# Gate and up projections as seven block products in a two-layer decoder trunk

## The chip, the cores and the metric

The kernel runs on one core of a Trainium2 chip. The metric is device time in microseconds (us) of one execution; the median of several runs is compared. The profile is of one further execution. Its engines are TensorE (PE, with PEld for its weight loads), VectorE (DVE), ScalarE (ACT), GpSimd (POOL) and SyncE (SP), which issues the loads.

## The reference

A decoder trunk of two layers on 512 tokens of width 1024, in float32. Each layer is a mixer (attention beside a convolution or a gated MLP) and a SwiGLU feed-forward network (FFN), each behind an RMS norm and with a residual. Only the FFN changes:

```
def swiglu(h, w_gate, w_up, w_down):          # h 512 x 1024, F = 2816
    gate = jnp.einsum('bsd,df->bsf', h, w_gate)
    up = jnp.einsum('bsd,df->bsf', h, w_up)
    return jnp.einsum('bsf,fd->bsd', jax.nn.silu(gate) * up, w_down)

h = h + swiglu(rms_norm(h, ffn_norm_g[layer]), ffn_w_gate[layer], ffn_w_up[layer], ffn_w_down[layer])
```

After the second layer the result goes through a last RMS norm.

## The kernel before

The residual stream is kept transposed: `h[k]`, k = 0 to 7, holds 128 features on the partitions and 512 tokens along the columns. Every float32 product is made of three fp32r products: each operand is split into a high part (a rounding copy on ScalarE) and a low part (a subtraction on VectorE), and hi·hi, hi·lo and lo·hi are added up in a PSUM bank (`acc3`, lines 181 to 187, and `mac` inside `tok_gemm`, lines 241 to 248).

The norm is deferred. `residual` (line 349) adds a product to `h[n]`, and `norm_tile` (line 292) at once splits g·h into `xh[n]` and `xl[n]`; the squares are summed in `nacc`. The scale itself comes later: `norm_a` sums the squares over features with eight short matmuls, and `norm_b` spreads the result over the partitions by transposes into `R`, by which every product is multiplied when it is read out of PSUM.

Weights arrive as one stream `ws` of 182 blocks of 128x1024 (512 KB) in the order of use. `dma_block` loads, three blocks ahead; `prep_unit` splits half a block (128x512, four weight tiles), three units ahead, with ScalarE for hi and, in the FFN, VectorE for lo (in the first mixer GpSimd makes lo).

The FFN (`ffn`) goes over 22 tiles of 128 hidden features. For each it makes the gate product over eight k tiles in one bank, then the up product in another, 24 matmuls of 512 columns each, feature-major: weights are stationary and tokens move, so that the hidden tile comes out with features on the partitions. `act` multiplies by `R`, applies silu, multiplies, and splits the hidden tile into `hh` and `hl`. When all 22 are there, the down projection follows: in layer 0 output tile by output tile over all 22 (528 matmuls), with `residual` and the split for the next mixer behind each; in layer 1 in `last_down`, token-major (`tok_gemm`), in two halves of 512 output columns, while `turn_h` transposes `h` between the matmuls; the last norm and the stores end the kernel.

TensorE runs in the written order; the other engines' orders are found by a planner at compile time. `Seq` puts dependent steps of the mixers between weight products at estimated times.

Of the kernel before, what the change touches and what calls it, by code (L numbers as in the profile page):

```python
# [10 lines left out]
def _warn_once_fixed(msg, *args, **kwargs):  # L11
# [12 lines left out]
P = 128  # L24
S = 512
# [54 lines left out]

def order_ffn_in():
    return [(w, k, f) for f in range(NF) for w in range(2) for k in range(KT)]


def order_down(layer):
    if layer == 0:
        return [(k, n) for n in range(8) for k in range(NF)]
    return [(k, 4 * half + j) for half in range(2) for k in range(NF) for j in range(4)]
# [23 lines left out]
NBLK = 182  # L112
TK = dict(schedule_with_timeline_sim=True)
# [4 lines left out]
def trunk_kernel(ctx: ExitStack, tc: tile.TileContext, xT, ws, cols, sinks, sgu_g, sgu_b,  # L118
# [23 lines left out]
    def dma_block():  # L142
        b = st["dma"]
        raw = wpool.tile([P, 1024], F32, name="raw", bufs=RAW_AHEAD)
        nc.sync.dma_start(raw, ws[b])
        raws[b] = raw
        st["dma"] += 1

    def prep_unit():
# [11 lines left out]
        if half:  # L161
            del raws[b]
            if st["dma"] < NBLK and st["dma"] <= b + RAW_AHEAD:
                dma_block()

    def next_unit():
        u = st["tile"] // 4
        while st["prep"] < min(2 * NBLK, u + PREP_AHEAD + 1):
            prep_unit()
# [19 lines left out]
    # ---- the order on TensorE: products of weights run on, steps that wait for other engines  # L189
    # are put between them when their operands should be there ----  # L190
# [158 lines left out]
    def residual(n, ps, gname):  # L349
        V.tensor_add(h[n], h[n], ps)  # L350
        norm_tile(n, gname)
# [26 lines left out]
    def pt_av(items, vap, rl, dst, banks, line="V", ta="TA", ao="AO"):  # L378
        """items: (unit, column AP of P, key block, first, last)."""
# [46 lines left out]
    # ================= layer 0 mixer =================  # L426
    with ExitStack() as mx:
# [18 lines left out]
        def conv_tile(j, pool_taps):  # L446
            """The first taps: products on ScalarE, summed on GpSimd; the others on VectorE in PSUM."""
# [24 lines left out]
        # GLU pairs  # L472
        def glu(j, pa, pb):
# [4 lines left out]
            # a * sigmoid(b) = a * (tanh(b / 2) + 1) / 2; the half is in the taps  # L478
# [9 lines left out]
        # what is done with a product once the norm's scale is known  # L488
# [37 lines left out]
        # keys: the high part of a head on both halves of the partitions, the low part on its own;  # L526
        # queries: high and low part stacked, so that one pass gives (q_hi + q_lo) k_hi
# [578 lines left out]
```

## Time and profile before

| | us |
|---|---|
| median of 3 runs (lowest to highest) | 1154.53 (1154.25 to 1156.39) |
| span of the profiled execution, first to last instruction | 1148.2 |
| own time of the profiled execution | not listed |
| TensorE busy | 1116.0 (97%) |
| VectorE, ScalarE, GpSimd busy | 596.3, 478.2, 172.8 |

The median lies 6.3 us above the span, for what comes ahead of the first and behind the last instruction. A busy TensorE says that matmuls were under way, not how fast they went: one is shown with 0.39 us while the next starts earlier, so the distance from start to start is the price of a matmul. The granted clock is shown as a share of 2.4 GHz; its other level is 1.2 GHz.

### The profile page before, as it was taken

Reading aid. Unit: us, or ns where it says so; the run is one execution under the profiler, and the core shown is the slowest. Engines: PE = TensorE matmul, PEld = TensorE weight load, DVE = VectorE, ACT = ScalarE, POOL = GpSimd, SP = SyncE. Lnnn points to the kernel's source line nnn. Section 1 sums busy time; section 2 is a strip of 40 time slices with the busy share of each in tenths; the row PEclk is TensorE's granted clock in tenths of the full one; section 3 lists DMA queues with packets and bytes.
Section 4 is the critical chain, followed back from the end, with each engine's and each line's share of the span. In section 5 each row is a group of like instructions: output and inputs, shape, how many; then the busy total and the mean of one; then the engine's idle time right before and its main releaser. Section 6 shows DMA issues by size and latency. Waiting matters only on the chain.

```text
span 1148.2 us, 13412 instructions
## 1 busy us (share of the span) xinstructions
PE 1116.0 (97%) x5132; PEld 911.2 (79%) x5132; DVE 596.3 (52%) x999; ACT 478.2 (42%) x848; POOL 172.8 (15%) x138
## 2 busy tenths in 40 slices
PE   6989899999999999999999999999999999999997
PEld 4867678888888888888887878788888888888886
DVE  6889776544444444333347545664454444432323
ACT  4577666433333333323346644444333333333323
POOL 4788654000000000000024100000000000000100
PEclk9989899999999999999999999999999999999999
DMA  5211112223223322322522111232222322332321
GB/s 212 85 62 56 37 37 92 93 95 106 93 92 98 105 91 92 110 93 92 166 91 71 40 37 52 80 107 88 96 92 95 107 92 92 104 100 91 106 96 74
DMA packets 31281, 103.92 MB, mean 91 GB/s; under 512 B 3568, under 2 KB 4464, under 8 KB 31216
## 3 DMA queue, kind: packets, MB, share of 16 engines
q1 hardware_dynamic: 31216, 103.06, 26.8%
q8 instruction: 40, 0.66, 0.2%
q14 instruction: 25, 0.20, 0.1%
HBM read 100.95 MB, written 2.10 MB: 90 GB/s over the span
## 4 chain that ended last, share of the span: by engine, by line
PE 89%; DVE 5%; POOL 2%; issue 2%; ACT 1%; DMA 0%; SPq 0%; POOLq 0%; ACTq 0%; DVEq 0%
PE bank L184 23%; PE bank L185 22%; PE bank L186 22%; PE bank L245 5%; PE bank L247 4%; PE bank L246 4%; PE bank L404 2%; PE bank L390 1%; PE bank L910 1%; POOL yc L458 1%; PE bank L909 1%; PE bank L567 1%; POOL w_lo L134 1%; PE bank L566 1%; DVE bank L462 0%
## 5 line engine op out<-in xcount | busy, mean ns | idle before, releaser
L157 ACT ACTIVATE w_hi<-raw 128x512 fp32r<-128x512 f32 x364 | 229.4, 631 | 461.7 <-PE bank L185 364.1
L184 PE MATMUL bank<-xh,w_hi 128*128 128x512 f32 x912 | 363.0, 398 | 6.6 <-ACT xh L296 6.6
L134 DVE TENSOR_TENSOR w_lo<-raw,w_hi 128x512 fp32r<-128x512 f32 x321 | 226.1, 705 | 268.7 <-ACT w_hi L157 268.5
L185 PE MATMUL bank<-xl,w_hi 128*128 128x512 f32 x912 | 359.3, 394 | 1.8 <-DVE xl L297 1.7
L186 PE MATMUL bank<-xh,w_lo 128*128 128x512 f32 x912 | 358.5, 393 | 0.0
L184 PEld LDWEIGHTS bank<-xh,w_hi 128*128 128x128 f32 x912 | 173.6, 190 | 44.1 <-ACT xh L296 6.6
L185 PEld LDWEIGHTS bank<-xl,w_hi 128*128 128x128 f32 x912 | 173.7, 190 | 39.2 <-DVE xl L297 4.0
L186 PEld LDWEIGHTS bank<-xh,w_lo 128*128 128x128 f32 x912 | 173.5, 190 | 36.4
L245 PE MATMUL bank<-w_hi,hh 128*128 128x512 f32 x176 | 69.4, 394 | 0.1
L247 PE MATMUL bank<-w_hi,hl 128*128 128x512 f32 x176 | 68.6, 390 | 0.0
L246 PE MATMUL bank<-w_lo,hh 128*128 128x512 f32 x176 | 68.5, 389 | 0.0
L184 PE MATMUL bank<-hh,w_hi 128*128 128x512 f32 x176 | 68.5, 389 | 0.0
L185 PE MATMUL bank<-hl,w_hi 128*128 128x512 f32 x176 | 68.5, 389 | 0.0
L186 PE MATMUL bank<-hh,w_lo 128*128 128x512 f32 x176 | 68.5, 389 | 0.0
L134 POOL TENSOR_TENSOR w_lo<-raw,w_hi 128x512 fp32r<-128x512 f32 x43 | 59.3, 1379 | 47.4 <-ACT w_hi L157 42.0
L756 DVE TENSOR_TENSOR gb<-bank,R 128x512 f32<-128x512 f32 x44 | 30.4, 691 | 64.7 <-PE bank L186 64.7
L754 DVE TENSOR_TENSOR ga<-bank,R 128x512 f32<-128x512 f32 x44 | 30.4, 692 | 63.6 <-PE bank L186 62.8
L458 POOL TENSOR_TENSOR yc<-yc,prod 128x512 f32<-128x512 f32 x44 | 59.3, 1348 | 8.6 <-ACT prod L457 7.3
L850 POOL TENSOR_SCALAR_AFFINE_SELECT wT<-wT 128x1024 f32<-128x1024 f32 x1 | 1.1, 1097 | 360.8 <-DMA wT<-in_spat_wT 360.8
L462 DVE SCALAR_TENSOR_TENSOR bank<-cp,cc,bank 128x512 f32<-128x512 f32 x72 | 54.0, 750 | 1.2
L346 ACT ACTIVATE hh<-gb 128x512 fp32r<-128x512 f32 x44 | 27.8, 632 | 61.5 <-DVE gb L757 61.4
L825 POOL TENSOR_TENSOR xh<-xh,xl 128x512 f32<-128x512 f32 x4 | 5.7, 1454 | 297.7 <-ACT sq L810 297.7
(175 smaller groups left out, 1344.8 us busy)
## 6 DMA issues: line engine op xcount, KB each, us to landing
raw<-in_ws SPq DMA_DIRECT2D x181, 512.0 KB, 3.4
h<-in_xT SPq DMA_DIRECT2D x8, 256.0 KB, 6.2
out_y<-xh SPq DMA_DIRECT2D x8, 256.0 KB, 2.2
raw<-in_ws SPq DMA_DIRECT2D x2, 256.0 KB, 3.5
ropeC<-in_rope_c SPq DMA_DIRECT2D x2, 256.0 KB, 4.1
ropeS<-in_rope_s SPq DMA_DIRECT2D x2, 256.0 KB, 5.1
wT<-in_spat_wT SPq DMA_DIRECT2D x1, 512.0 KB, 6.2
xl<-in_fin_g SPq DMA_DIRECT2D x2, 256.0 KB, 3.7
```

The source lines that it names most:

```text
L134: eng.tensor_tensor(out=out, in0=a, in1=b, op=ALU.subtract)
L157: A.activation(hi, src, AF.Copy)
L184: T.matmul(ps, hi, xh, start=start, stop=False)
L185: T.matmul(ps, hi, xl, start=False, stop=False)
L186: T.matmul(ps, lo, xh, start=False, stop=stop)
L245: T.matmul(ps[t], xh[:, c], hi, start=(k == 0), stop=False)
L246: T.matmul(ps[t], xh[:, c], lo, start=False, stop=False)
L247: T.matmul(ps[t], xl[:, c], hi, start=False, stop=(k == last))
L458: G.tensor_add(yc[j], yc[j], p)
L462: V.scalar_tensor_tensor(acc, src, w, acc, op0=ALU.mult, op1=ALU.add)
L754: V.tensor_mul(g, pg, R)
L756: V.tensor_mul(u, pu, R)
```

## The change

The gate and up products of a group of four hidden tiles (512 features; the last group has two) become one block product: tokens 0 to 255 and 256 to 511 are the two row blocks, the two halves of the 1024 input features the inner blocks, gate and up the two column blocks. Strassen's scheme in Winograd's form makes it from seven products instead of eight. The sums of activation blocks (S1 to S4) are made once a layer by `sums`, and those of weight blocks (T1 to T4) once a group: T1 and T3 on GpSimd, T2 and T4 on VectorE, in place in the loaded blocks. The sums of products are taken partly in PSUM (banks are added to by a second product after a copy of their first state) and partly on VectorE. The products are token-major, the split activations stationary, and the weights move with 512 columns (256 in the last group).

The hidden features so come out with tokens on the partitions, and `turn` transposes them for the down projection. That is now made group by group, added to `h` each time, between the second and third product of the next group; the last two groups go together at the end, in layer 1 in `last_down`. The norm's scale is a per-token column, so `norm_b` is not called in the FFN. Weights of the FFN's first part no longer pass through `prep_unit`: they have eight buffers of their own (`raw2`, of which the scaled activations take four at first), and are split 1024 columns at a time into three pairs of buffers. `residual` ahead of the FFN no longer splits g·h; the FFN does. The diff's removal of comments is left out below, as are the layout of the weights in memory and the small edits of the stream.

```diff
+GROUPS = [list(range(4 * g, min(4 * g + 4, NF))) for g in range((NF + 3) // 4)]
+BLOCKS = ((0, 0), (1, 0), (1, 1), (0, 1))
+EARLY_N = 3
...
-    def residual(n, ps, gname):
+    def residual(n, ps, gname=None):
         V.tensor_add(h[n], h[n], ps)
-        norm_tile(n, gname)
+        if gname:
+            norm_tile(n, gname)
+        else:
+            norm_sq(n)
...
+    PRODUCTS = (("B11", "A11", 0), ("T1", "S1", 1), ("T2", "S2", 0), ("B22", "S4", 1),
+                ("T3", "S3", 0), ("B21", "A12", 2), ("T4", "A22", 0))
...
+            def operand(name, q, src=None):
...
+                A.activation(hi, src, AF.Copy)
+                sub(V, lo, src, hi)
...
+            def sums(q, x1, x2):
+                a11, a21, a12, a22 = x1[:, :, :256], x1[:, :, 256:], x2[:, :, :256], x2[:, :, 256:]
+                s1, s2, s3, s4 = [scr.tile([P, 2, 256], F32, name=x) for x in ("ga", "gb", "ga", "gb")]
+                sub(V, s1, a22, a21)
+                operand("S1", q, s1)
+                V.scalar_tensor_tensor(s2, s1, -1.0, a11, op0=ALU.mult, op1=ALU.subtract)
+                operand("S2", q, s2)
+                V.scalar_tensor_tensor(s4, s2, -1.0, a12, op0=ALU.mult, op1=ALU.subtract)
+                operand("S4", q, s4)
+                sub(V, s3, a11, a21)
+                operand("S3", q, s3)
+                operand("A12", q, a12)
+                operand("A22", q, a22)
...
+                    x = xg[kh, q] = fp.tile([P, 2, S], F32, name="raw2", bufs=8)
+                    for i in range(2):
+                        k = 4 * kh + 2 * q + i
+                        A.activation(x[:, i, :], h[k], AF.Copy, scale=col(gname, k))
+                    if kh == 0:
+                        operand("A11", q, x[:, :, :256])
+                    else:
+                        sums(q, xg[0, q], x)
...
+            def source(g, name, q):
...
+                    into, more, eng = {"T1": ("B11", "B12", G), "T2": ("T1", "B22", V),
+                                       "T3": ("B12", "B22", G), "T4": ("T2", "B21", V)}[name]
+                    t, other = source(g, into, q), source(g, more, q)
+                    eng.tensor_add(t, t, other)
...
+            def prep_op():
...
+                hi = fp.tile([P, 1024], F32R, name="w2h", bufs=3)
+                lo = fp.tile([P, 1024], F32R, name="w2l", bufs=3)
+                A.activation(hi, src, AF.Copy)
+                sub(V, lo, src, hi)
...
+            def product(g, p, ps, start):
...
+                        for t in range(2):
+                            c = slice(t * P, (t + 1) * P)
+                            out = ps[t][:, :w]
+                            T.matmul(out, xh[:, j % 2, c], wh, start=(start and j == 0), stop=False,
+                                     skip_group_check=True)
+                            T.matmul(out, xh[:, j % 2, c], wl, start=False, stop=False, skip_group_check=True)
+                            T.matmul(out, xl[:, j % 2, c], wh, start=False, stop=(j == 3),
+                                     skip_group_check=True)
...
+            def turn(g, src, half):
...
+                for t in range(2):
+                    pt = bank(6 + t)
+                    for i in range(n):
+                        T.transpose(pt[:, i * P:(i + 1) * P], src[t][:, i * P:(i + 1) * P], ident)
+                    pv = pt[:, :n * P].rearrange("p (f c) -> p f c", f=n)
+                    c = slice((2 * half + t) * P, (2 * half + t + 1) * P)
+                    A.activation(hh[:, :, c], pv, AF.Copy)
+                    sub(V, hl[:, :, c], pv, hh[:, :, c])
...
+                    if prev is not None and p == 0:
+                        turn(g - 1, prev["u2"], 0)
+                    if prev is not None and p == 1:
+                        turn(g - 1, prev["p5"], 1)
+                    product(g, p, banks[b], p in (0, 1, 5))
+                    if p == 1:
+                        if g == 0:
+                            norm_a(7)
+                        elif g < last:
+                            for n in range(8):
+                                pd = bank(6 + n % 2)
+                                down(g - 1, n, pd, True, True)
+                                V.tensor_add(h[n], h[n], pd)
...
+                        if p == 0:
+                            A.activation(p1, ps[t], AF.Copy)
+                        elif p == 1:
+                            A.activation(p5, ps[t], AF.Copy, scale=-1.0)
+                        elif p == 2:
+                            A.activation(u2, ps[t], AF.Copy, scale=-1.0)
+                        elif p == 3:
+                            sub(V, u2, u2, ps[t])
+                        elif p == 4:
+                            sub(V, p5, p5, ps[t])
+                        elif p == 5:
+                            V.tensor_add(p1, p1, ps[t])
+                            A.activation(p1, p1, AF.Silu, scale=r[0])
+                            V.scalar_tensor_tensor(u2, u2, r[0], p1, op0=ALU.mult, op1=ALU.mult)
+                        else:
+                            A.activation(g2, ps[t], AF.Silu, scale=r[1])
+                            V.scalar_tensor_tensor(p5, p5, r[1], g2, op0=ALU.mult, op1=ALU.mult)
+                    if layer == 1 and g == last and p in (4, 5, 6):
+                        turn_h(p - 4)
```

## Rows read from the trace of the kernel before

**Rows 1.** The page: busy time by engine, granted clock in 40 slices (tenths).

```profile
PE 1116.0 (97%) x5132; PEld 911.2 (79%) x5132; DVE 596.3 (52%) x999; ACT 478.2 (42%) x848; POOL 172.8 (15%) x138
...
PEclk9989899999999999999999999999999999999999
```

**Rows 2.** Windows of the gate and up stages; columns stand in the first line.

```profile
core 0: us, PE busy (x) PEld busy (x) DVE busy (x) ACT busy (x) POOL busy (x), PEclk, DMA share, GB/s
...
199.20:452.00 252.80, 252.80 (x1124) 209.48 (x1124) 121.74 (x188) 89.64 (x143) 2.13 (x2) 1.00 0.29 97
...
776.00:1018.00 242.00, 242.00 (x1077) 200.51 (x1075) 115.11 (x178) 86.20 (x136) 1.01 (x1) 1.00 0.29 98
```

**Rows 3.** Timeline of TensorE (start, duration), feature-major; 27 triples apart.

```profile
540.46 0.39 PE L184 MATMUL bank<-hh,w_hi 128*128 128x512 f32 x1
...
558.82 0.39 PE L184 MATMUL bank<-hh,w_hi 128*128 128x512 f32 x1
```

**Rows 4.** The same view, token-major in the last down projection; 11 triples apart.

```profile
1124.95 0.39 PE L245 MATMUL bank<-w_hi,hh 128*128 128x512 f32 x1
...
1132.43 0.39 PE L245 MATMUL bank<-w_hi,hh 128*128 128x512 f32 x1
```

**Rows 5.** The same view around the norm's broadcast, eight transposes.

```profile
787.95 1.05 PE L339 MATMUL bank<-ident,rc 128*128 128x128 f32 x8
788.76 0.48 PE L184 MATMUL bank<-xh,w_hi 128*128 128x512 f32 x1
789.08 0.39 PE L185 MATMUL bank<-xl,w_hi 128*128 128x512 f32 x1
```

**Rows 6.** The same view, score matmuls of 256 columns in the first mixer.

```profile
91.58 0.38 PE L567 MATMUL bank<-kl,qs 64*128 64x256 f32 x1
91.89 0.38 PE L566 MATMUL bank<-khh,qs 128*128 128x256 f32 x1
```

**Rows 7.** The same view around four transposes of h.

```profile
1019.80 0.60 PE L798 MATMUL bank<-ident,h 128*128 128x128 f32 x4
1020.15 0.48 PE L245 MATMUL bank<-w_hi,hh 128*128 128x512 f32 x1
1020.47 0.39 PE L246 MATMUL bank<-w_lo,hh 128*128 128x512 f32 x1
```

**Rows 8.** Groups by line and form: total, mean ns, idle before, by releaser.

```profile
L157 ACT ACTIVATE w_hi<-raw 128x512 fp32r<-128x512 f32 x364 | 229.4, 631 | 461.7 <-PE bank L185 364.1 <-PE bank L247 80.7 <-issue 8.1
...
L913 DVE CUSTOM_DVE_ANT_0 Pm<-bank,mask 128x512 f32<-128x512 f32 x8 | 5.4, 688 | 1.8 <-PE bank L910 1.7
...
L913 DVE CUSTOM_DVE_ANT_0 Pm<-bank,mask 128x256 f32<-128x256 f32 x8 | 3.3, 422 | 2.6 <-PE bank L910 2.3
```

**Rows 9.** Timeline of VectorE at the first layer's FFN entry.

```profile
189.75 1.79 DVE L319 TENSOR_TENSOR nacc<-nacc,sq 128x512 f32<-128x512 f32 x1
...
193.31 1.33 DVE L319 TENSOR_TENSOR nacc<-nacc,sq 128x512 f32<-128x512 f32 x1
...
202.05 0.68 DVE L319 TENSOR_TENSOR nacc<-nacc,sq 128x512 f32<-128x512 f32 x1
202.65 0.68 DVE L134 TENSOR_TENSOR w_lo<-raw,w_hi 128x512 fp32r<-128x512 f32 x1
203.25 0.74 DVE L297 SCALAR_TENSOR_TENSOR xl<-h,cc,xh 128x512 fp32r<-128x512 f32 x1
```

**Rows 10.** Timeline of GpSimd in the same stretch.

```profile
189.67 1.31 POOL L134 TENSOR_TENSOR w_lo<-raw,w_hi 128x512 fp32r<-128x512 f32 x1 [2.11 <-ACT w_hi L157]
192.80 1.30 POOL L134 TENSOR_TENSOR w_lo<-raw,w_hi 128x512 fp32r<-128x512 f32 x1 [1.81 <-ACT w_hi L157]
```

**Rows 11.** Windows ahead of the two FFNs; columns as in rows 2.

```profile
760.00:776.00 16.00, 16.00 (x72) 13.24 (x71) 10.01 (x15) 7.31 (x12) 0.00 (x0) 1.00 0.29 98
...
188.00:199.20 11.20, 11.20 (x50) 9.19 (x50) 11.14 (x15) 7.75 (x14) 4.09 (x4) 1.00 0.23 71
```

**Rows 12.** The page: loads of weight blocks, KB each, us to landing.

```profile
raw<-in_ws SPq DMA_DIRECT2D x181, 512.0 KB, 3.4
```

**Rows 13.** Window and timeline of TensorE behind a wait in the first mixer.

```profile
66.00:70.00 4.00, 1.77 (x5) 1.15 (x5) 3.94 (x10) 3.63 (x8) 4.00 (x4) 0.59 0.16 40
...
69.82 0.63 PE L185 MATMUL bank<-xl,w_hi 128*128 128x512 f32 x1
70.25 0.63 PE L186 MATMUL bank<-xh,w_lo 128*128 128x512 f32 x1
```

More of the change, by code (lines that the diff above doesn't have):

```diff
@@ L112 @@
 NBLK = 182
+SIZES = (14, 8, 44, 22, 20, 8, 44, 22)
+STARTS = [sum(SIZES[:i]) for i in range(len(SIZES) + 1)]
+STREAM = [b for i in range(len(SIZES)) if i % 4 != 2 for b in range(STARTS[i], STARTS[i + 1])]
 TK = dict(schedule_with_timeline_sim=True)
@@ L784, in last_down, with hidden, temps @@
-    def last_down(hid):
+            fp = fx.enter_context(tc.tile_pool(name="ffn", bufs=1, reuse_waits="tile"))
+            last = len(GROUPS) - 1
+            gname = f"ffn_g{layer}"
+            hid = {}
+            def hidden(g):
+                end = "z" if g == last else ""
+                hid[g] = [fp.tile([P, len(GROUPS[g]), S], F32R, name=f"h{x}{end}") for x in "hl"]
+            def temps():
+                return {"p1": [scr.tile([P, S], F32, name="ga") for _ in range(2)],
+                        "p5": [scr.tile([P, S], F32, name="gb") for _ in range(2)],
+                        "u2": [fp.tile([P, S], F32, name="ta", bufs=2) for _ in range(2)],
+                        "g2": [fp.tile([P, S], F32, name="tb", bufs=2) for _ in range(2)]}
@@ new lines, in ffn @@
+            xg = {}
+            for kh in range(2):
+                for q in range(2):
+                    x = xg[kh, q] = fp.tile([P, 2, S], F32, name="raw2", bufs=8)
[6 more added lines that the diff above has]
+                        sums(q, xg[0, q], x)
@@ new lines, in ffn, with block @@
+            base = STARTS[4 * layer + 2]
+            order = [(g, p, q) for g in range(last + 1) for p in range(7)
+                     for q in range(2 if len(GROUPS[g]) == 4 else 1)]
+            fs = dict(block=0, prep=0, take=0)
+            blocks, made, ops = {}, {}, {}
+            def block(g, name, q):
+                nq = 2 if len(GROUPS[g]) == 4 else 1
+                want = 8 * g + BLOCK_OF[name] * nq + q
+                while fs["block"] <= want:
+                    raw = fp.tile([P, 1024], F32, name="raw2", bufs=8)
+                    nc.sync.dma_start(raw, ws[base + fs["block"]])
+                    blocks[fs["block"]] = raw
+                    fs["block"] += 1
+                return blocks[want]
@@ new lines, in ffn @@
+            if gnext is not None:
+                pd = {n: bank(n) for n in range(EARLY_N)}
+                for n in range(EARLY_N):
+                    down(last - 1, n, pd[n], True, False)
+                    if n < 2:
+                        turn(last, prev["u2" if n == 0 else "p5"], n)
+                for n in range(8):
+                    if n < EARLY_N:
+                        down(last, n, pd[n], False, True)
+                    else:
+                        pd[n] = bank(n % 6)
+                        down(last - 1, n, pd[n], True, False)
+                        down(last, n, pd[n], False, True)
+                    residual(n, pd[n], gnext)
+            else:
+                hidden(last)
+                xs2 = [(hid[g][0][:, i, :], hid[g][1][:, i, :]) for g in (last - 1, last)
+                       for i in range(len(GROUPS[g]))]
+                last_down(xs2, lambda k: turn(last, prev["u2" if k == 0 else "p5"], k) if k < 2 else None)
@@ new lines, in trunk_kernel, with turn_h, last_down @@
+    ht_ = []
+    def turn_h(part):
+        if not ht_:
+            ht_.extend([keep.tile([P, S], F32, name=f"xh{2 * t + f}") for f in range(2)] for t in range(NQ))
+        for i in ((0, 1, 2), (3, 4, 5), (6, 7))[part]:
+            f, t = divmod(i, NQ)
+            pt = bank(6 + i % 2)
+            for j in range(4):
+                T.transpose(pt[:, j * P:(j + 1) * P], h[4 * f + j][:, t * P:(t + 1) * P], ident)
+            A.activation(ht_[t][f], pt, AF.Copy)
+    def last_down(hid, each):
```

130 lines of the change are left out of this document (74 added, 56 removed).

## Prediction

> **What bounds the kernel now.** I read the first part of the page, then the windows by stage, then the timeline of TensorE, because the question is whether any time in the two SwiGLU stages is not TensorE's. TensorE is busy for 97% of the span, VectorE for 52%, GpSimd for 15%, at the full clock almost everywhere [rows 1]. In the windows of the gate and up products TensorE has no gap at all: 252.80 of 252.80 us and 242.00 of 242.00 us, with VectorE at 48% and GpSimd idle but for one or two instructions [rows 2]. So these stages last as long as their matmuls do.
>
> The price of a matmul is the distance between starts, since the shown 0.39 us overlap. In a run of feature-major products 27 triples (hi·hi, hi·lo, lo·hi) take from 540.46 to 558.82 us: 0.680 us a triple, 0.2267 us a matmul of 512 columns [rows 3]. Token-major ones, as the change uses, go at the same rate: 11 triples from 1124.95 to 1132.43 us, 0.680 us [rows 4]. Their form costs nothing.
>
> **What the products save.** Before, a layer has 22 tiles x 2 matrices x 8 k tiles x 3 = 1056 matmuls, 239.4 us. After, a block product is 4 k tiles x 2 token tiles x 3 = 24 matmuls, and a group has seven. Five groups of four tiles: 840 of 512 columns, 190.4 us. The last group has two tiles: 168 of 256 columns. No uniform stream of that width is in the trace. Eight transposes of 128 columns before a full-width matmul take 0.81 us, 0.10 each [rows 5]; 512 columns take 0.227, which is 0.213 for the columns at 2.4 GHz and 0.013 over. I take 0.107 + 0.013 = 0.120 us, 20.2 us in all, between bounds of 0.10 (16.8 us) and 0.227 (38.1 us). A row of 256 columns at 0.31 us exists [rows 6], but there full-height and half-height weights alternate, which the change never does; it is only a far upper end. A layer goes from 239.4 to 210.6 us: **-28.8 each, -57.6 us in all** (between -64 and -22).
>
> **What TensorE gets to do instead.** The hidden tiles come out with tokens on the partitions and have to be turned: per full group 16 transposes in two calls of `turn`. The transposes of `h` now show the price: four take 1019.80 to 1020.15, 0.35 us, and the first matmul behind them has 0.32 instead of 0.23 us to the next start, so 0.44 us per four [rows 7]. Eight in a row: 0.81 and 0.09, as the broadcast of the norm shows [rows 5]. That makes 0.9 x 10 + 0.44 x 2 = 9.7 us a layer: **+19.4 us**. The broadcast itself (`norm_b`) leaves both FFNs: 0.90 x 2, **-1.8 us**. The down projection keeps its 528 matmuls a layer; only their order changes. `turn_h` keeps its 32 transposes, but three in a row go through two PSUM banks and wait for ScalarE's copies: +1. TensorE's own balance is -57.6 + 19.4 - 1.8 + 1 = **-39.0 us**.
>
> **Who feeds it now.** The weights of a product are 128x1024 pieces, split into hi on ScalarE and lo on VectorE; a piece feeds 12 matmuls, 2.72 us. VectorE takes 0.688 us at 512 columns and 0.422 at 256 [rows 8]: 1.04 ns a column, so 1.22 us at 1024. ScalarE at 0.63 us for 512 needs at most 1.26, and is half idle. Per full group VectorE then has 14 splits (17.1), four sums T2 and T4 (4.9), six readings of PSUM (4.1), four gated products (3.0, at 0.75 as the three-operand split of `xl` in [rows 9]) and four splits behind the transposes (2.8): 31.9 us beside 39.9 us of products and transposes. Groups 1 to 4 also contain 21.8 us of down matmuls, in which VectorE has only 16 instructions of 0.69. Three buffers let VectorE run two pieces ahead, 5.4 us less the 2.5 us of a split. On average that holds, and starts of 512-column instructions lie 0.60 us apart in a queue [rows 9], so 31.9 is on the high side.
>
> Against it stands GpSimd, which makes T1 and T3. While a GpSimd subtraction ran from 189.67 for 1.31 us, a VectorE addition of two SBUF operands started at 189.75 and took 1.79 us; at 192.80 and 193.31 the same, 1.33 us. Undisturbed it takes 0.68 [rows 9, 10]. Both times VectorE ended 0.55 us behind GpSimd's end: it stood still until GpSimd was through. The Trainium skill, "SBUF — State Buffer", section "SBUF: two separate sides", says so: the port pair that both share is an exclusive lock for the whole instruction, against a VectorE instruction with two SBUF inputs. By that rule every lo split and every operand sum is exposed to every T1 and T3; if such instructions ran freely side by side, the stall term below would be near half. The trace agrees with the rule.
>
> T1 and T3 are four additions of 1024 columns a group. From 1.31 us at 512 [rows 10] I take 2.6 us each (1.3 if most were fixed), 10.4 us a group. In groups 1 to 4, T3 can run under the down matmuls; T1 falls at the group's start, where the readings of two products and a turn come together: about 5.3 us of VectorE work and 2.6 of GpSimd per 5.4 us of matmuls. Two pieces ahead hide most of it. I take 0.7 us of stall at each of the ten group changes, 7 us (0 to 3 us each), and 1 us in each narrow last group, where a product is only 2.9 us long: 2 us.
>
> **Group 0** is the weak place; no down product gives time back. VectorE also makes the sums of the activations there: per half 10 instructions of 0.69 and the split of A11, 15.2 us a layer. Without them it has 29.1 us before the first turn, with them 44.3, and GpSimd up to 10.4 more, against 38.1 us of matmuls. Before group 0 begins VectorE is not free: 10.01 of 16 us busy at the second layer's entry, 11.14 of 11.20 at the first [rows 11]. What leaves it there is the split of eight `xl` tiles. The last residual lands only after the first matmul of the FFN could start; S1, S2 and S4 of the second half hang on it, one after the other. B22's loads also wait for buffers that the scaled activations hold, and a load takes 3.4 us [rows 12]. With some 8 us done ahead and half of GpSimd's time beside PSUM reads, 44.3 + 5 - 8 = 41.3 against 38.1, and order adds to it: I take 4 us at the second layer and 6 at the first, where weights may also wait for the mixer's memory: 10 us (2 to 25).
>
> Stalls: 7 + 2 + 10 = **+19 us**. Sum: -39.0 + 19 = **-20.0 us**, and the span goes from 1148.2 to 1128.2 us. The own time of the profiled execution is not listed; the median of the timed runs is 6.3 us above its span, which I carry over: **1134.5 us**. The 8 to 10 us of ScalarE work that group 0 adds for scaling and splitting cost nothing, because ScalarE is busy 42% of the span; with no cover they would lengthen the 10 us term.
>
> **Rivals.**
> 1. *Everything hidden.* The look-ahead absorbs the lock and the entries. Stalls 0 to 9 us; 1115.5 to 1124.5 us. For it: VectorE's average load of 80% in the products and the 0.60 us spacing [rows 9]. Against it: 11.14 of 11.20 us at the first entry [rows 11].
> 2. *Slower: the port bounds the products.* Each T1 and T3 holds VectorE for its full 2.6 us and look-ahead does not recover it. A full group then needs 31.9 + 10.4 = 42.3 against 39.9 us; group 0 44.3 + 10.4 = 54.7 against 38.1. That is 16.6 + 5 x 2.4 = 28.6 us a layer, 57.2 in all: -39.0 + 57.2 = +18.2, 1172.7 us. It decides from 19.5 us of stall a layer. For it: the two locked additions [rows 9, 10]. Against it: the down matmuls between, during which VectorE catches up.
> 3. *The narrow group is no cheaper.* Its 168 matmuls take 0.227 us each like wide ones: 2 x 17.9 = +36 us, less the 2 us of stall that they then hide, 1168 us; half way, at 0.17 us, 1152. For it: only the 256-column row [rows 6]. Against it: the transposes at 0.10 us [rows 5, 7].
>
> **How the numbers follow.** The forecast's case (stalls of 10 to 30 us, 1125 to 1145 us) gets 0.50, rival 1 0.27, rival 2 from its point on 0.13, rival 3 0.06, half of it on either side, and 0.04 lies on the line. A change of 0.2% (2.3 us) is about what a measurement of this kernel can tell from none. Faster: 0.50 + 0.27 + 0.03 = 0.80; within 0.2%: 0.04; slower: 0.13 + 0.03 = 0.16. The range for 8 in 10 goes from 1112, half way from the sum without stalls (1115.5) to the same with narrow matmuls at 0.10 us (1109), to 1156, where rival 2 has just overtaken the gain; the likeliest case's own is 1125 to 1145.
>
> **What would show it.** Right: 840 matmuls a layer 0.227 us apart and 168 at 0.12; pieces of 1024 columns at 1.2 us on VectorE; TensorE idle mostly in the first 45 us of each FFN, waiting for lo splits or sums; VectorE splits beside GpSimd's additions stretched to 2 or 3 us. Wrong: TensorE without gaps there (rival 1), gaps in every group at its start (rival 2), the last group at 0.2 us a matmul (rival 3). What would upset all of it is an idle stretch long enough that the granted clock falls: between 66 and 70 us, with TensorE busy for 1.77 of 4.00 us behind a wait for VectorE, it was 0.59 on average, that is partly at 1.2 GHz, and matmuls of 512 columns started 0.43 us apart, from 69.82 to 70.25 [rows 13].

## Result, and the profile after

The changed kernel takes 1227.11 us (median of 5 runs, 1219.61 to 1227.53) against 1154.25 us: a ratio of 1.0624 [1.059, 1.0659] (in brackets the 95% interval, here and below), slower. The forecast was 1134.5 us with 0.80 on faster. The profiled execution has a span of 1217.5 us (own time 1219.61, the shortest of the five), 69.3 more than before.

The page of the kernel after, the lines that answer to [rows 1]:

```profile
PE 1111.9 (91%) x5196; PEld 905.9 (74%) x5196; DVE 839.0 (69%) x1105; ACT 573.0 (47%) x932; POOL 317.6 (26%) x182
...
PEclk9989998899999999999999999988999999999999
```

TensorE was busy for 97% and is now for 91%; the clock, without a dip there in [rows 1], dips in slices 7 and 8 and 27 and 28, where the two FFNs begin. The windows of the two FFNs, from the mixer's last matmul to the last down matmul or the end, answer to [rows 2]:

```profile
core 0: us, PE busy (x) PEld busy (x) DVE busy (x) ACT busy (x) POOL busy (x), PEclk, DMA share, GB/s
197.20:594.60 397.40, 360.30 (x1635) 297.15 (x1634) 287.25 (x305) 172.89 (x243) 72.82 (x23) 0.95 0.26 88
810.58:1217.50 406.92, 363.44 (x1665) 300.63 (x1664) 280.69 (x298) 176.87 (x254) 81.55 (x31) 0.95 0.25 86
```

Before, the first FFN lasted 360.9 us without a gap. Now TensorE is busy for about as long (360.3), at a mean clock of 0.95, and stands still for 37 us besides. From the last matmul of a mixer to that of the FFN's down projection, and in layer 1 to the last matmul of all, the kernel before takes 360.92 + 365.16 = 726.1 us and this one 397.19 + 399.89 = 797.1: +71.0 us. The mixer between them takes 215.9 and 216.0. The first mixer ended anywhere from 196.8 to 204.0 us in the profiled executions of this study, so experiments are compared below by this sum of the two FFNs ("FFN sum") as well as by their times.

The sum of the prediction without stalls would be 726.1 - 39.0 = 687.1; the stalls are 110 us, not 19. They lie in two places, in both layers: from the mixer's last matmul to the end of group 0, and at every change of group. The page's groups name the instructions that stretch (mean ns of one behind the comma):

```profile
L147 DVE TENSOR_TENSOR w2l<-raw,w2h 128x1024 fp32r<-128x1024 f32 x154 | 227.1, 1475 | 103.2 <-ACT w2h L864 103.1
L854 POOL TENSOR_TENSOR raw<-raw,raw 128x1024 f32<-128x1024 f32 x44 | 134.6, 3065 | 583.7 <-DVE w2l L147 582.3
```

**A change of group.** The three timelines of layer 0 from the last product of group 2 into group 3 (GpSimd, VectorE, TensorE), and a window behind the wait.

```profile
394.61 5.65 POOL L854 TENSOR_TENSOR raw<-raw,raw 128x1024 f32<-128x1024 f32 x2 [56.03 <-DVE w2l L147]
401.41 5.58 POOL L854 TENSOR_TENSOR raw<-raw,raw 128x1024 f32<-128x1024 f32 x2 [1.16 <-DVE w2l L147]
```
```profile
393.30 1.23 DVE L147 TENSOR_TENSOR w2l<-raw,w2h 128x1024 fp32r<-128x1024 f32 x1 [0.30 <-ACT w2h L864]
394.44 3.55 DVE L953 SCALAR_TENSOR_TENSOR ta<-ta,rc,ga 128x512 f32<-128x512 f32 x2
397.92 3.42 DVE L147 TENSOR_TENSOR w2l<-raw,w2h 128x1024 fp32r<-128x1024 f32 x1
401.26 3.54 DVE L956 SCALAR_TENSOR_TENSOR gb<-gb,rc,tb 128x512 f32<-128x512 f32 x2
404.72 3.36 DVE L147 TENSOR_TENSOR w2l<-raw,w2h 128x1024 fp32r<-128x1024 f32 x1
408.00 1.27 DVE L147 TENSOR_TENSOR hl<-bank,hh 128x512 fp32r<-128x512 f32 x2
```
```profile
403.82 0.39 PE L892 MATMUL bank<-w2h,xl 128*128 128x512 f32 x1
408.74 1.71 PE L904 MATMUL bank<-ident,gb 128*128 128x128 f32 x8 [4.53 <-DVE hl L147]
410.10 0.78 PE L889 MATMUL bank<-w2h,xh 128*128 128x512 f32 x1
410.67 0.63 PE L891 MATMUL bank<-w2l,xh 128*128 128x512 f32 x1
411.10 0.63 PE L892 MATMUL bank<-w2h,xl 128*128 128x512 f32 x1
...
413.01 0.40 PE L891 MATMUL bank<-w2l,xh 128*128 128x512 f32 x1
```
```profile
408.70:413.00 4.30, 4.26 (x15) 3.50 (x16) 4.26 (x5) 2.03 (x3) 0.00 (x0) 0.60 0.01 4
```

The four additions of T1 and T3 all run here, in two pairs, each released by a `w2l` split of B11, into whose tile T1 is added. Until 408.0 VectorE's turns alternate with GpSimd's: a split of 1.22 us takes 3.42, two gated products (1.41 undisturbed) 3.55. The two splits end at 401.34 and 408.08, 1.08 and 1.09 us behind the end of a pair of additions (400.26 and 406.99): each has stood until GpSimd was through and then run. The `hl` split of the first turn is behind them in VectorE's queue and starts at 408.00. Its source, PSUM banks 6 and 7, is what the second turn writes to, so TensorE stands for 4.5 us. Then its matmuls start 0.43 us apart instead of 0.227, as in [rows 13], until 412.8: the second level of the clock, 0.60 on average from 408.7 to 413.0 in the last row above (last column but two). A group from turn to turn is 68.4 us long (329.03 to 397.45), where 61.7 would do (below): 6.7 us each, some 4.7 of it standing and 2 at half clock.

**The entry.** ScalarE's timeline behind the first mixer, and TensorE's (its last mixer matmul starts at 197.17), and two windows:

```profile
197.96 4.38 ACT L821 ACTIVATE raw<-h,cc 128x512 f32<-128x512 f32 x7
...
202.76 0.71 ACT L821 ACTIVATE raw<-h,cc 128x512 f32<-128x512 f32 x1
203.38 1.14 ACT L797 ACTIVATE xh<-raw 128x512 fp32r<-128x512 f32 x2
204.42 1.04 ACT L864 ACTIVATE w2h<-raw 128x1024 fp32r<-128x1024 f32 x1
```
```profile
205.51 0.80 PE L889 MATMUL bank<-w2h,xh 128*128 128x512 f32 x1 [7.95 <-ACT w2h L864]
```
```profile
197.40:205.50 8.10, 0.16 (x1) 0.00 (x0) 5.26 (x10) 8.07 (x14) 0.00 (x0) 0.73 0.85 328
205.50:212.00 6.50, 5.54 (x14) 4.05 (x15) 6.50 (x10) 5.07 (x9) 4.67 (x1) 0.55 0.47 166
```

All eight scalings of `h` come in one block after the mixer's last matmul, although seven of the eight tiles of `h` had been final since 196.2 (the last residual starts at 197.67), and the first weights' split stands behind them: in these 8.1 us ScalarE (the fourth engine in the windows) is busy for 8.07. TensorE starts at half clock (0.55 from 205.5 to 212.0), and group 0 then takes 55.1 us (205.51 to 260.60) for 38.1 us of matmuls.

### The profile page after: what moved, and what is told of

Its sections match the earlier page's. It is cut to its first block, busy times and chain, and to the rows that moved or that the text cites. A ratio compares the mean times of both kernels' runs of the same rounds, so it can differ in the third digit from the quotient of the medians.

```text
span 1217.5 us, 13823 instructions
## 1 busy us (share of the span) xinstructions
PE 1111.9 (91%) x5196; PEld 905.9 (74%) x5196; DVE 839.0 (69%) x1105; ACT 573.0 (47%) x932; POOL 317.6 (26%) x182
## 4 chain that ended last, share of the span: by engine, by line
PE 71%; DVE 16%; issue 5%; POOL 4%; ACT 3%; DMA 0%; SPq 0%; POOLq 0%; DVEq 0%; ACTq 0%
PE bank L197 11%; PE bank L198 10%; PE bank L199 10%; PE bank L891 9%; PE bank L889 8%; PE bank L892 8%; DVE w2l L147 4%; DVE gb L956 3%; DVE ta L953 2%; PE bank L420 2%; PE bank L258 2%; PE bank L260 2%; PE bank L259 2%; POOL raw L854 2%; PE bank L904 1%
## 5 line engine op out<-in xcount | busy, mean ns | idle before, releaser
L147 DVE TENSOR_TENSOR w2l<-raw,w2h 128x1024 fp32r<-128x1024 f32 x154 | 227.1, 1475 | 103.2 <-ACT w2h L864 103.1
L854 POOL TENSOR_TENSOR raw<-raw,raw 128x1024 f32<-128x1024 f32 x44 | 134.6, 3065 | 583.7 <-DVE w2l L147 582.3
L864 ACT ACTIVATE w2h<-raw 128x1024 fp32r<-128x1024 f32 x154 | 162.4, 1057 | 218.5 <-PE bank L892 123.9
L889 PE MATMUL bank<-w2h,xh 128*128 128x512 f32 (+1 forms) x384 | 155.5, 405 | 21.4 <-ACT w2h L864 21.4
L891 PE MATMUL bank<-w2l,xh 128*128 128x512 f32 (+1 forms) x384 | 152.9, 398 | 9.8 <-DVE w2l L147 9.8
L892 PE MATMUL bank<-w2h,xl 128*128 128x512 f32 (+1 forms) x384 | 151.5, 394 | 0.1
L147 DVE TENSOR_TENSOR w_lo<-raw,w_hi 128x512 fp32r<-128x512 f32 x145 | 103.8, 717 | 58.7 <-ACT w_hi L170 56.8
L197 PE MATMUL bank<-xh,w_hi 128*128 128x512 f32 x208 | 87.7, 422 | 5.7 <-ACT xh L309 5.7
L198 PE MATMUL bank<-xl,w_hi 128*128 128x512 f32 x208 | 84.9, 408 | 2.5 <-DVE xl L310 2.3
L199 PE MATMUL bank<-xh,w_lo 128*128 128x512 f32 x208 | 83.6, 402 | 0.0
```

Source lines behind the costliest of these rows:

```text
L147: eng.tensor_tensor(out=out, in0=a, in1=b, op=ALU.subtract)
L197: T.matmul(ps, hi, xh, start=start, stop=False)
L198: T.matmul(ps, hi, xl, start=False, stop=False)
L199: T.matmul(ps, lo, xh, start=False, stop=stop)
L854: eng.tensor_add(t, t, other)
L864: A.activation(hi, src, AF.Copy)
```

## Experiments

The first four kernels start from the changed one, e5, e8 and e10 from e4, e6 from e5, and e11 from e10. The kernel before ran beside each.

**e1_sums_on_vector.** T1 and T3 on VectorE.

```diff
-                    into, more, eng = {"T1": ("B11", "B12", G), "T2": ("T1", "B22", V),
-                                       "T3": ("B12", "B22", G), "T4": ("T2", "B21", V)}[name]
+                    into, more, eng = {"T1": ("B11", "B12", V), "T2": ("T1", "B22", V),
+                                       "T3": ("B12", "B22", V), "T4": ("T2", "B21", V)}[name]
```

> T1 and T3 are added on VectorE instead of GpSimd. Theory (GpSimd's additions, 3.07 us each in the changed kernel, hold up VectorE's instructions on two SBUF operands, and TensorE then waits 4.5 us at the second turn of a group): the wait falls to at most 1.5 us a group, the lo splits of 1024 columns go from a mean of 1.48 to about 1.22 us, a full group from 68.4 to about 62.5 us, and the time falls by 45 to 65 us, to 1160 to 1180 us. Rival (VectorE simply has too much work at the change of a group, on whichever engine the sums are made): its 4 x 1.22 us more work a group come on top, a full group takes 70 us or more, and the time is 1227 us or above.

Measured: 1159.38 us (1157.07 to 1160.94), ratio 1.0069 [1.0049, 1.0089]; FFN sum 734.0. VectorE has 54 us more to do and the kernel is 68 us faster. The wait at the second turn is gone; a group takes 62.7 us. GpSimd's help cost more than the work that it took away.

**e2_no_t1_t3.** T1 and T3 left out.

```diff
-                    eng.tensor_add(t, t, other)
+                    if eng is not G:
+                        eng.tensor_add(t, t, other)
```

> T1 and T3 are left out (B11 and B12 are used in their place, so part of the computation is missing); nothing else changes. It bounds what the two sums cost wherever they are made. Theory of the hold-up: about 5 to 10 us below the kernel with the sums on VectorE, with no wait over 1 us at the turns; what is left above the time before is the entries of the two FFNs. Rival (too much work on VectorE otherwise): the turns still wait 2 us or more, and the time stays within 20 us of the changed kernel.

Measured: 1133.89 us (one run), span 1132.0, FFN sum 713.5. A group takes 61.66 us: no stall is left in it. What remains is the entry, with 7.95 and 7.90 us for the first `w2h`. The 20.5 us to e1 are the additions' own price on VectorE: 8 x 1.07 in the full groups, and most of the rest in the two groups 0, where e1 waits 2.99 and 1.02 us for `w2l` and e2 0.30.

**e3_turn_banks.** The second turn gets other PSUM banks; GpSimd keeps T1 and T3.

```diff
-                        turn(g - 1, prev["p5"], 1)
+                        turn(g - 1, prev["p5"], 1, banks[2])
```

> The second turn of a group writes the free third pair of PSUM banks instead of the pair that the first turn has just used; GpSimd keeps its sums. Theory, second half (TensorE waits because the first turn's lo splits, late in VectorE's queue, still hold banks 6 and 7): the wait of 4.5 us at the second turn goes to 1 us or less, as its own input is ready some 4 us before those splits end; with the clock's loss behind it 5 to 6 us a full group, 40 to 50 us in all, to about 1180 us, unless the down matmuls then wait for the same splits. Rival (the late gated product is what the second turn waits for): the wait moves there and stays at 4 us, and the time is within 10 us of the changed kernel.

Measured: 1206.38 us (1201.95 to 1208.55), ratio 1.0464 [1.043, 1.0499]. The wait for `hl` is gone, but 2.4 us of it stand a little later:

```profile
409.68 0.50 PE L891 MATMUL bank<-w2l,xh 128*128 128x512 f32 x1 [2.42 <-DVE w2l L147]
```

A group takes 66.7 us, a gain of 1.7 of the 6.7. The banks were only the first place where a late VectorE showed; the weights' lo splits are the next in its queue. The gain is about half of what was expected.

**e4_vector_and_banks.** e1 and e3 together.

```diff
+                    into, more, eng = {"T1": ("B11", "B12", V), "T2": ("T1", "B22", V),
+                                       "T3": ("B12", "B22", V), "T4": ("T2", "B21", V)}[name]
...
+                        turn(g - 1, prev["p5"], 1, banks[2])
```

> Both: the sums on VectorE and the second turn in the third pair of banks. Theory: no wait of TensorE at any group change; a full group at 61.7 us (24 matmuls x 7 and 96 of the down projection at 0.2267, and 1.8 for the turns); what is left is the two entries and the first groups. Time 1155 to 1170 us. If VectorE's load is what matters, as much slower as with the sums on VectorE alone.

Measured: 1152.91 us (1146.59 to 1157.43), ratio 1.0004 [0.9981, 1.0027]; FFN sum 726.5, before 726.1. The same place as above, VectorE and TensorE:

```profile
381.87 1.41 DVE L953 SCALAR_TENSOR_TENSOR ta<-ta,rc,ga 128x512 f32<-128x512 f32 x2
...
384.33 1.22 DVE L147 TENSOR_TENSOR w2l<-raw,w2h 128x1024 fp32r<-128x1024 f32 x1
...
390.19 1.28 DVE L147 TENSOR_TENSOR hl<-bank,hh 128x512 fp32r<-128x512 f32 x2
```
```profile
391.24 1.04 PE L904 MATMUL bank<-ident,gb 128*128 128x128 f32 x8
392.03 0.48 PE L889 MATMUL bank<-w2h,xh 128*128 128x512 f32 x1
```

From the first gated product to `hl` it is 8.3 us, three weight sums among them; with GpSimd's help it was 13.6 without these. A group takes 61.66 us and has no wait. So the -39.0 us of TensorE's balance are now eaten by the entries alone: from the mixer's last matmul to the end of group 0 it is 57.6 us (204.00 to 261.59) and 59.2 in the second layer, for 38.1 of matmuls each. In the kernel after, the same stretches take 63.4 and 62.1: 8.8 us of its loss there went with GpSimd's additions.

**e8_idle_additions.** e4 with eight additions a full group on GpSimd that nobody reads.

```diff
                             V.scalar_tensor_tensor(u2, u2, r[0], p1, op0=ALU.mult, op1=ALU.mult)
+                            if w == S:
+                                idle = scr.tile([P, S], F32, name="R", bufs=1)
+                                for _ in range(4):
+                                    G.tensor_add(idle, u2, u2)
```

> As e4_vector_and_banks, with eight additions of 128x512 by GpSimd in every full group, put behind the product of silu and u2, whose results nobody reads (additional work, none left out). Theory (what costs is GpSimd's presence at the memory beside VectorE's instructions with two operands in SBUF, not the wait for GpSimd's result): VectorE's w2l splits and the products of silu stretch from 1.2 us towards 2 to 3.5 us where they fall into those additions, waits on w2l or on the second turn come back, and the time rises by 15 to 60 us over e4's 1152.9. Rival (the cost was that T2 and the splits wait for T1 and T3 from a slow engine): nobody waits for these, so the time stays within 5 us of e4's.

Measured: 1209.89 us (1206.85 to 1211.34), ratio 1.0516 [1.0497, 1.0534]; FFN sum 784.1, 57.6 more than e4. Nobody waits for GpSimd here, and VectorE is held all the same, exactly as long as the additions run (GpSimd, then VectorE):

```profile
393.83 14.21 POOL L957 TENSOR_TENSOR R<-ta 128x512 f32<-128x512 f32 x8 [53.89 <-DVE ta L953]
```
```profile
391.80 1.23 DVE L147 TENSOR_TENSOR w2l<-raw,w2h 128x1024 fp32r<-128x1024 f32 x1 [0.30 <-ACT w2h L864]
...
396.26 2.06 DVE L147 TENSOR_TENSOR w2l<-raw,w2h 128x1024 fp32r<-128x1024 f32 x1
...
405.09 2.06 DVE L147 TENSOR_TENSOR w2l<-raw,w2h 128x1024 fp32r<-128x1024 f32 x1
407.07 1.28 DVE L147 TENSOR_TENSOR hl<-bank,hh 128x512 fp32r<-128x512 f32 x2
409.40 1.21 DVE L147 TENSOR_TENSOR w2l<-raw,w2h 128x1024 fp32r<-128x1024 f32 x1
```

The sums of 1.22 us on VectorE in this stretch take 2.06 like the splits, while the two `hl` at 407.07, which read PSUM, take their usual 1.28 beside the last addition. A full group is back at 67.2 to 68.3 us. At the group changes the cause is GpSimd's presence, not the lateness of its sums; the rival falls.

**e5_entry_direct.** e4; A11 is split straight from `h` into tiles outside the FFN's pool, and the weights of the first product come by rows through the mixer's stream.

```diff
+                    A.activation(hi[:, i, :], h[k][:, :256], AF.Copy, scale=g)
+                    V.scalar_tensor_tensor(lo[:, i, :], h[k][:, :256], g, hi[:, i, :],
+                                           op0=ALU.mult, op1=ALU.subtract)
...
+                        if stream:
+                            wh, wl = next_row()
```

> The sums on VectorE and the second turn in banks of the group, as in e4_vector_and_banks; besides, A11 is split straight from h into the tiles that live outside the feed-forward pool, and the weights of the first product of group 0 are read row by row as in the mixer, so that the first product needs neither the seven scalings by ScalarE nor the first w2h. Theory (the pool of the feed-forward stage lies on the mixer's memory, so ScalarE's scalings begin only with the mixer's last matmul and TensorE stands still for 8 us per layer): the idle 8 us before the first product shrinks to about 2 us, some of it comes back as a wait for T1's or S1's splits at the second product, and the time falls by 5 to 12 us over both layers, to about 1140 to 1148. Rival (the entry is bound by the loads of the weights, which land no earlier): the wait only changes its name to a DMA, and the time stays within 4 us of e4's 1152.9.

Measured: 1145.25 us (1143.32 to 1150.64), ratio 0.9961 [0.9942, 0.998]; FFN sum 722.2, 4.3 less than e4. The first product now starts without a gap, at 199.65, but the idle time went to the second one: 7.35 us for `w2h` and 5.58 for `w2l`. The time was as expected, the waits were not. TensorE, ScalarE and VectorE:

```profile
212.61 0.80 PE L911 MATMUL bank<-w2h,xh 128*128 128x512 f32 x1 [7.35 <-ACT w2h L881]
218.99 0.80 PE L913 MATMUL bank<-w2l,xh 128*128 128x512 f32 x1 [5.58 <-DVE w2l L148]
```
```profile
200.38 4.39 ACT L840 ACTIVATE raw<-h,cc 128x512 f32<-128x512 f32 x7
...
211.52 1.04 ACT L881 ACTIVATE w2h<-raw 128x1024 fp32r<-128x1024 f32 x1
```
```profile
207.08 1.23 DVE L871 TENSOR_TENSOR raw<-raw,raw 128x1024 f32<-128x1024 f32 x1 [0.40 <-DMA raw<-in_ws]
...
217.72 1.22 DVE L148 TENSOR_TENSOR w2l<-raw,w2h 128x1024 fp32r<-128x1024 f32 x1
```
```profile
200.40:212.60 12.20, 4.86 (x22) 3.70 (x20) 9.49 (x15) 12.20 (x23) 0.00 (x0) 0.92 0.83 308
206.00:230.00 24.00, 11.05 (x38) 8.34 (x39) 23.60 (x32) 14.88 (x24) 0.00 (x0) 0.72 0.45 159
```

The first wait is ScalarE's. The first half of T1 is added up at 208.31, but its `w2h` begins at 211.52, behind the eight scalings and the high parts of the operands; ScalarE is busy for all of the 12.20 us from 200.4 to 212.6. The second wait is VectorE's: from 206 to 230 us it (third in the windows) is full, TensorE (first) half empty, GpSimd idle.

**e6_entry_reordered.** e5, and group 0 begins with the two products that need no sums, both by rows.

```diff
-                for p, (_, _, b) in enumerate(PRODUCTS):
+                for p in (0, 5, 1, 2, 3, 4, 6) if g == 0 else range(7):
+                    b = PRODUCTS[p][2]
```

> As e5_entry_direct, and group 0 takes its products in the order A11.B11, A12.B21, then the five that need sums; the first two both read their weights by rows and both X blocks straight from h. The sums of X and of the weights then have two products, about 11 us, to be made in. Theory (group 0's 49 us against 39 is VectorE late with sums and splits, and the granted clock that falls after the waits): the waits of 3 us on w2l in group 0 go, the clock stays at 1.0, and the time falls to about 1125 to 1140, below both kernels. Rival (VectorE has more work in group 0 than TensorE whatever the order, so the wait only moves to later products): within 4 us of e5.

Measured: 1150.75 us (1147.96 to 1155.31), ratio 1.0008 [0.9991, 1.0025]; FFN sum 726.5. This is not what was expected: TensorE waits at 206.3 for ScalarE's `w_hi` (2.76), and for VectorE at 209.8 (`w_lo`, 2.99) and at 228.0 (the lo split of an S operand, 5.62). The order moves the waits. What does not fit seems to be the amount of work that ScalarE and then VectorE have around the first products; that is read from the waits and was not tried by itself.

**e10_group0_plain.** e4; group 0 of each layer in eight block products, without Strassen, its operands split straight from `h` and its weights taken by rows through the mixer's stream.

```diff
+            def eight():
+                for kh in range(2):
...
+                    for j in range(4):
+                        row(("A11", "A21") if kh == 0 else ("A12", "A22"), j, ps, kh)
...
+            def row(names, j, ps, kh):
+                wh, wl = next_row()
+                for t in range(4):
+                    xh, xl = xop[names[t // 2], j // 2]
...
-            order = [(g, p, q) for g in range(last + 1) for p in range(7)
+            order = [(g, p, q) for g in range(1, last + 1) for p in range(7)
```

> As e4_vector_and_banks, but group 0 of each layer is computed without Strassen: eight block products, the four blocks of X split straight from h, the weights by rows through the stream that the mixer uses, the gate for all four token tiles first and then the value. It costs TensorE one block product more, 5.4 us per layer, and takes from VectorE the sums of the weights (four of 1.2 us per layer), half of the splits of X before the first product, and the late sums: S1 to S4 are then made during group 0, not before it. Theory (the 56 us from the mixer's last matmul to the first group change in e5 are VectorE's: 206 to 230 us there it is busy without a gap, while TensorE waits 7.4 and 5.6 us and then runs at half clock): the stretch shrinks from 56.5 to 46 to 50 us, no wait above 2 us is left in it, the granted clock stays at 1.00, and the time is 1125 to 1135 us, below both kernels. Rival (the entry waits for the memory of the mixer's pool, for loads or for the last residual, whatever the products are): the waits stay at 10 us or more per layer and the extra product makes it 1145 to 1158 us.

Measured: 1120.79 us (1120.25 to 1122.45), ratio 0.9726 [0.9701, 0.9751]: faster than both kernels, 2.7% under the one before. FFN sum 700.0. Page and windows:

```profile
PE 1084.6 (97%) x5244; PEld 894.1 (80%) x5244; DVE 767.7 (69%) x1145; ACT 562.6 (50%) x944; POOL 174.4 (16%) x138
...
PEclk9999899999999999999999999999999999999999
```
```profile
206.00:230.00 24.00, 24.00 (x112) 19.96 (x111) 23.41 (x33) 16.98 (x29) 1.40 (x1) 1.00 0.54 187
```

In the same 24 us VectorE is as full as in e5, and TensorE has no gap: the sums that it worked on are now not needed before group 1. Group 0 ends 45.8 us behind the mixer (196.86 to 242.69), for 192 matmuls of 0.227 = 43.5. The one wait of over 0.5 us at the two entries is 0.82 us, for the last tile of `h`. The run changes three things at once (no sums, operands straight from `h`, weights past the FFN's buffers), so it shows that the entry can be filled, and not how much each of them gives; e5, with parts of the last two, gave 4.3 us of the 26.5 between e4 and e10.

**e11_plain_gpsimd.** e10's group 0, with T1 and T3 on GpSimd and, from group 2 on, the old banks for the second turn.

```diff
-                        turn(g - 1, prev["p5"], 1, banks[2])
+                        turn(g - 1, prev["p5"], 1, banks[2] if g == 1 else None)
```

> As the changed kernel (T1 and T3 on GpSimd, the second turn in the banks of the first), but with group 0 of each layer as in e10_group0_plain. It tells whether the two losses add up. Theory (two separate causes: 23 us a layer from the mixer's end to the end of group 0, and 27 us plus 5 in the narrow group at the group changes, where GpSimd holds VectorE): group 0 of each layer comes out at 46 to 50 us without a wait above 2 us, the full groups stay at 67 to 69 us, and the time is 1227 - 2 x (23 - 5.4) = 1192, between 1180 and 1198 us. Rival (both come from GpSimd, or from TensorE's clock carried over from the entry into the groups): the full groups shrink too, below 65 us, and the time falls below 1170 us.

Measured: 1186.26 us (1184.3 to 1188.89), ratio 1.0302 [1.0268, 1.0335]; FFN sum 760.5. From group 2 on the full groups are at 68.2 us (316.60 to 384.84), with the wait of 4.55 us for `hl` in each. Group 1 takes 61.6 (254.99 to 316.60): its four additions now run under group 0 (GpSimd, then VectorE, whose splits of 0.68 us stretch):

```profile
218.69 11.62 POOL L903 TENSOR_TENSOR raw<-raw,raw 128x1024 f32<-128x1024 f32 x4 [0.39 <-DVE w2l L149]
```
```profile
219.61 2.90 DVE L149 TENSOR_TENSOR w_lo<-raw,w_hi 128x512 fp32r<-128x512 f32 x1
222.43 2.88 DVE L149 TENSOR_TENSOR xl<-ga,xh 128x512 fp32r<-128x512 f32 x1
```

Group 0 so takes 51.5 and 51.3 us (e10: 45.8 and 45.0), with a wait of 2.55, both a little over what was expected. The time is as expected, and the two losses are separate: the entry's wait of 8 us is gone here too, and the additions of a full group cost 5.7 to 6.6 us in either place.

## Why the prediction was wrong

**TensorE's own balance was right.** -39.0 us, plus one more block product in each of the two layers (2 x 24 x 0.227 = 10.9), makes the FFN sum of e10 726.1 - 39.0 + 10.9 = 698.0; it measured 700.0. That leaves 2 us for all its stalls. The narrow group is as cheap as was assumed; in the kernel after, 43 distances of 256-column matmuls from 552.33 to 557.49 are 0.120 us each:

```profile
552.33 0.28 PE L889 MATMUL bank<-w2h,S3h 128*128 128x256 f32 x1
...
557.49 0.28 PE L891 MATMUL bank<-w2l,A12h 128*128 128x256 f32 x1
```

Rival 3 falls. The turns are 0.79 to 0.81 us each, and the pieces of 1024 columns take 1.22 us on VectorE, as predicted.

**The term that failed is the stalls: +19 was 110.** By places:

| | predicted | measured |
|---|---|---|
| ten group changes and the narrow groups | 7 + 2 | 8 x 6.7 + 2 x 4.9 = 63.4 |
| group 0 with the entry, both layers | 10 (2 to 25) | 46.6 (the rest of 110) |

(A full group without stall is 61.66 us long, the last group of layer 0 up to its own first turn 24.64, both as in e2.) e11 bears out the sizes place by place: over e10 it has six full groups with 6.6 us, two narrow ones with 4.4, and 12.0 in the two stretches up to the first turn, 60.4 in all, and its FFN sum is 60.5 more than e10's 700.0.

**At the group changes** the step that failed is "two pieces ahead hide most of it". The lock was read from [rows 9, 10] and sized fairly: GpSimd's addition took 2.8 us at the median (3.07 on average, with its worst in group 0) instead of 2.6, some of it its own wait, and VectorE lost 13.6 - 8.3 and the 3 x 1.13 of the sums that e4 makes besides, 8.7 us a change or 2.2 an addition. But the prediction spread T1 and T3 over the group ("T3 can run under the down matmuls"). The trace has all four within 12.4 us, from 394.61 to 406.99, on top of the gated products and the turn, where VectorE has the most instructions with two operands in SBUF. A look-ahead of two pieces is worth 5.4 us of matmuls; VectorE lost more than that in one go, and the first to suffer was not a weight split but the `hl` of the turn, which has no look-ahead at all. Rival 1 (everything hidden) falls with it. Rival 2 had the mechanism and the sign, and its mark, gaps in every group at its start, is what the trace shows. Its price was too low (2.4 us a group, 57.2 in all), although it allowed VectorE's loss 10.4 us where 8.7 were measured, because it balanced loads over a group: between the changes VectorE does catch up, as the rival's "against" says, and TensorE cannot get back what it has lost.

The Trainium skill, "SBUF — State Buffer", section "SBUF: two separate sides", counts VectorE's instructions with two SBUF inputs among those that the lock concerns, and has it held for the whole instruction. The trace agrees with both: beside GpSimd's additions `w2l` goes from 1.22 to 3.42 us and ends 1.08 us behind an addition's end, while in e8 `hl`, one of whose inputs is in PSUM, takes 1.28 us for two beside an addition as without one.

**At the entry** the prediction had the right place and about a fifth of the size. Three steps failed. First, "some 8 us done ahead": nothing is done ahead. The scalings and the first `w2h` all come after the mixer's last matmul; the tiles of the FFN's pool take over memory of the mixer's. That this holds them back is likely, since e5's A11, in tiles outside that pool, is split from 187.37 on, but it was not tried by itself. Secondly, ScalarE's 8 to 10 us of scaling and splitting "cost nothing, because ScalarE is busy 42% of the span". Here it is busy for 8.07 of the first 8.1 us, and TensorE waits 7.95 and 7.90 us for it; in e5, where the first product does not need it, the second waits 7.35 for it. Thirdly, VectorE's 44.3 us against 38.1 were taken as an average that order only adds to; in fact most of it (sums, splits of S) is due before the second product. The 46.6 us are such waits and the half clock behind them; 8.8 of them go with GpSimd's additions (e4), and how the rest divides between ScalarE and VectorE stays open. e5 and e6 show that neither an earlier first product nor another order of products helps much; e10, in which the sums are due only in group 1, some 45 us later, removes the stall.

**The clock** was named as what would upset all of it, and had a part. In both FFNs of the kernel after it falls at the entry (0.55 on average from 205.5 to 212.0, 0.50 from 818.6 to 825.1) and behind the wait of 4.5 us at a turn (0.60 from 408.7 to 413.0), where it is about 2 us of each 6.7. Such a stall is dearer than the wait that the trace lists. Behind e3's wait of 2.42 us the matmuls were 0.24 us or less apart again from the second on, at a granted clock of 1.00 (409.68 to 412.00).

**The 6.3 us carried over** from the span to the median were too much: the runs of this study have 1.7 to 2.1 us between the span and the own time of an execution. Executions of the kernel before with a span of 1148.2 us took 1149.9 and 1150.0, so its profile was of an execution faster than the median.

## What to carry to other kernels

Before work is given to GpSimd, ask what VectorE runs at that moment with two operands in SBUF, and not what share of GpSimd is free: here taking 135 us of additions away from it, onto an engine that was already 69% busy, gained 68 us. An engine's mean share says as little of what it can take on: ScalarE, busy for 42% of the span before, was what TensorE waited for first at each entry. Load balances over a stage say little; at each point where several short chains meet (a group change, a stage's entry), add up what is due there and follow it to the instruction without look-ahead. Where a cheaper algorithm needs preparation, run the first portion with the plain one, and prepare beneath it.

## What the runs showed of the hardware

One GpSimd addition of 1024 columns cost the VectorE instruction with two SBUF operands beside it 2.2 us, at 512 columns as at 1024: 3.42 less 1.22 for a split of 1024 columns, 3.55 less 1.41 in a pair of gated products, 2.90 less 0.68 for a split of 512 (e11). In e8, additions of 512 columns cost 0.84 us each (2.06 less 1.22); they read one tile twice, so that the two prices are not of the same kind of addition. A subtraction of 512 columns of two tiles had cost 1.11 (1.79 less 0.68, [rows 9, 10]).

The time shown for an instruction contains its wait for the other engine, on GpSimd too: e8's additions show 1.78 us on average (14.21 for eight), where each VectorE instruction lost 0.84. The longest wait is GpSimd's:

```profile
L854 POOL TENSOR_TENSOR raw<-raw,raw x44: 2342/2802/9245, 207.3 to 1145.6; 128x1024 f32<-128x1024 f32 x44
```

The longest addition of the kernel after, 9.2 us, is the first of group 0, at 207.33. VectorE's instructions beside it, one behind the other until 214.36, take their usual 0.68 and 1.21 us, and the addition ends 2.2 us behind the last of them. Why VectorE kept its place there and gave way at the group changes, these runs do not show.

From one matmul to the next it was 4.9 us at 403.82 to 408.74, and after the transposes there the matmuls went 0.43 us apart until 412.8 and then 0.23 again; at e10's entry it was 1.20 us (197.56 to 198.76), and the matmuls were 0.24 or less apart from the second one on.
